# Weight slots of 2304 bytes: the 64-byte shift moves from the activation sums to the weights of the seven-product jobs

## The chip, the cores and the metric

The kernel runs on one core of a Trainium2 chip. The metric is the device time of one execution in microseconds (us); a lower time is better. The kernel before was timed three times: 955.7, 956.73 and 957.67 us, so its median is 956.73 us.

## What is computed

One layer of a decoder for 512 positions of width 1024, in float32:

```python
h = rmsnorm(x, norm_mix_g)
bg, cg, xv, q, k, v, z, a, b, ga, gb = split(h @ w_in)
y_a = (bg * causal_dwconv(cg * xv, conv_a_w)) @ w_a_out
y_b = gdn_branch(q, k, v, z, a, b, ...) @ w_b_out      # gated delta rule, 8 heads, chunks
x = x + (sigmoid(ga) * y_a + sigmoid(gb) * y_b) @ w_o
h = rmsnorm(x, norm_ffn_g)
gate, val = split(causal_dwconv(h @ w_up, ffn_conv_w))
x = x + (silu(gate) * val) @ w_down
out = rmsnorm(x, norm_final_g)
```

The products with `w_in`, `w_up`, `w_o`, `w_down`, `w_a_out` and `w_b_out` make up nearly all of the work.

## The kernel before

**Three matmuls for one.** Each float32 operand of a large product is split into a rounded part (type fp32r) and the rest, and a product becomes high times low, low times high and high times high (`mm3`, `times`). Activations are split once (`hT`, `h2`, `yas`, `yb`, `mix`, `xs`; the trace names `h2` as `h`). Weights are split as they pass: a block of 1 MB is loaded by an SP DMA into one of two `raw` tiles, and `Block.part` lets ACT round each quarter of 2048 bytes per partition into a `wh` slot (line 140) and DVE subtract it into a `wl` slot (line 141). There are `WQ` = 12 slots of each kind, used in a ring: a quarter's slot is written again when TensorE has read it for the last time. SP, ACT and DVE each take their instructions in order.

**Jobs.** `run_jobs` walks a list of pairs (block, use). During job i, one step of the split of block i+1 is put out at each tick, and a tick falls after every 2048 streamed columns (`mm`). Loads are issued some jobs ahead. There are three kinds of jobs:

- `col_job`: a 256-column block of weights against all 512 positions, 48 matmuls with 512 streamed columns and the weights stationary. Its block has four quarters.
- `sum_job`: the same result by seven products of half-size blocks instead of eight (Winograd's form of Strassen's method). Each product is 12 matmuls with 256 streamed columns, so a job has 84. Its block (`SumBlock`) splits seven parts, "11", "22", "s2", "s1", "s3", "s4" and "12". Three of the products, "11", "s4" and "12", stream quarters of the activations themselves (`hT` or `h`), and the other four stream the sums of such quarters, which `activation_sums` makes once for each stage: the tiles `ts` in the first stage and `us` in the stage of `w_up`. There are ten sum jobs in the first stage (three each of `w_in`'s columns cg, bg and ga, and one of xv) and eight in the stage of `w_up`.
- the jobs of `w_o` and `w_down` (`FormBlock`, `times_a`, `times_b`): activations are stationary here, and the weights stream with 512 columns.

**Where tiles lie.** In bytes within a partition, the program before has the `wh` slots from 19424 on and the `wl` slots from 44000 on, 2048 apart; the halves of `hT` at 68576 and 84960, those of `h` at 84960 and 101344; the tiles of `ts` at 134624 and 151264 and those of `us` at 151008 and 167648. All these numbers leave 224 when divided by 256. `place` makes the tiles of `ts` and `us`, which are 64 elements longer than their contents; for these two names alone the contents begin `UP` = 48 elements (192 bytes) into the tile:

```python
UP = 48
def place(pool_, tag, name, up=0):
    t = pool_.tile([P, ND * S + 64], F32R, tag=tag, name=name)[:, up:up + ND * S]
```

So the distance from the address of a streamed quarter of `hT` or `h` to that of any weight of 128 columns is a multiple of 256 bytes, and for `ts` and `us` it is 192 more than a multiple of 256.

**Between the stages.** The last jobs of `w_o` finish rows of x, normalise them (`fin1`), turn them on TensorE and write `h` (lines 1375 and 1376). The first two blocks of `w_up` are used together by `first_val`, on one half of the positions and then on the other, with 256 streamed columns. `activation_sums` (lines 251, 258, 260 and 261) then makes `us`.

**The order on each engine.** The code puts instructions out as the queues of tasks advance at ticks, and the framework's planner orders each engine's instructions by its own costs except where the code says otherwise.

Of the kernel before, what the change touches and what calls it, by code (L numbers as in the profile page):

```python
# [28 lines left out]
Y_V, Y_T, Y_G, Y_N, Y_E, SLAB = 4, 17, 16, 3, 4, 4  # L29
Y_F = (5, 4, 6, 3)  # L30
WARM = 3
WQ = 12
FEED = 3
Y_M = 10

# [25 lines left out]
def layer_kernel(ctx, tc, x, norm_mix_g, w_in, w_ab, conv_a_w, gdn_conv_w, gdn_A_log, gdn_dt_bias,  # L61
# [60 lines left out]
            mm(o, ah, bh, False, i == n - 1, free)  # L122


    class Block:
        def __init__(self, src, quarter=(4, P)):
            self.src, self.quarter = src, quarter
            self.raw, self.ready, self.lead, self.fed = None, False, 2, True
            self.wh, self.wl = {}, {}
# [5 lines left out]
            nc.sync.dma_start(out=self.raw, in_=self.src())  # L135

        def part(self, name, src):
            wh = self.wh[name] = wp.tile([P, *self.quarter], F32R, tag="wh", bufs=WQ, name=nm("wh"))
            wl = self.wl[name] = wp.tile([P, *self.quarter], F32R, tag="wl", bufs=WQ, name=nm("wl"))
            act.copy(out=wh, in_=src)  # L140
            dve.tensor_tensor(out=wl, in0=src, in1=wh.bitcast(F32), op=ALU.subtract)  # L141

# [8 lines left out]


    class SumBlock(Block):
        def split(self):
            if self.ready:
                return
            self.ready = True
            r = [self.raw[:, q] for q in range(4)]

            def to(q, a, b, op):  # L160
                dve.tensor_tensor(out=r[q], in0=a, in1=b, op=op)  # L161

            self.part("11", r[0])
            yield
            self.part("22", r[2])
            yield
            to(2, r[3], r[2], ALU.add)
            to(3, r[0], r[3], ALU.subtract)
            yield
            to(0, r[2], r[0], ALU.subtract)  # L170
            self.part("s2", r[0])
            yield
            self.part("s1", r[2])
            yield
            self.part("s3", r[3])
            yield
            to(0, r[1], r[0], ALU.subtract)
            self.part("s4", r[0])
            yield
            self.part("12", r[1])  # L180
            yield
# [146 lines left out]
        return SumBlock(lambda: w[i]), use  # L328


    UP = 48

    def place(pool_, tag, name, up=0):
        t = pool_.tile([P, ND * S + 64], F32R, tag=tag, name=name)[:, up:up + ND * S]
        return t.rearrange("p (m a n) -> p m a n", m=4, a=4)

    def by_rows(t):
# [101 lines left out]
    with tc.tile_pool(name="st1", bufs=1) as st1:  # L439
# [83 lines left out]
                                     op0=ALU.mult, op1=ALU.subtract)  # L523

        def round_k(q):
            wh = k_block.wh[q] = wp.tile([P, 4, P], F32R, tag="wh", bufs=WQ, name=nm("wh"))
            act.copy(out=wh, in_=k_block.raw[:, q])

        def rest_k(q):
            wl = k_block.wl[q] = wp.tile([P, 4, P], F32R, tag="wl", bufs=WQ, name=nm("wl"))  # L530
            dve.tensor_tensor(out=wl, in0=k_block.raw[:, q], in1=k_block.wh[q].bitcast(F32), op=ALU.subtract)


# [89 lines left out]
    def gates_chain(o):  # L623
        abT = gd.tile([P, S], F32, tag="cv", bufs=2, name="abT")[0:32]
        act.copy(out=abT, in_=o[0:32, :])
        yield
        o2 = bank()
        for n in range(NT):
            pe.transpose(out=o2[:, n * 32:(n + 1) * 32], in_=abT[:, n * P:(n + 1) * P], identity=ident[:32, :32])
        ab4 = o2[:, 0:128].rearrange("p (n c) -> p c n", c=32)  # L630
        abv = gd.tile([P, 16, NT], F32, name="abv")
        dve.tensor_copy(out=abv, in_=ab4[:, 16:32])
        dve.tensor_tensor(out=abv, in0=abv, in1=ab4[:, 0:16], op=ALU.add)
        T = lambda n: gd.tile([P, 32], F32, tag=n, name=nm(n))
        u, t, z, q, g = T("u"), T("t"), T("z"), T("q"), T("g")
        dve.tensor_tensor(out=hn(u), in0=abv[:, 0:8, :], in1=dtb.unsqueeze(2).broadcast_to([P, H, NT]), op=ALU.add)
        tc.keep_in_program_order(act.activation(out=hn(beta), in_=abv[:, 8:16, :], func=AF.Exp, scale=-1.0))
        tc.keep_in_program_order(act.activation(out=alg, in_=alg, func=AF.Exp))
        dve.tensor_scalar(t, u, -1.0, None, op0=ALU.mult)
        dve.tensor_tensor(out=t, in0=t, in1=u, op=ALU.min)  # L640
        tc.keep_in_program_order(act.activation(out=t, in_=t, func=AF.Exp))
        yield
        pool.tensor_scalar(beta, beta, 1.0, None, op0=ALU.add)
        pool.tensor_scalar(z, t, 2.0, None, op0=ALU.add)
        yield
        dve.reciprocal(out=beta, in_=beta)
        dve.reciprocal(out=z, in_=z)
        dve.tensor_scalar(u, u, 0.0, None, op0=ALU.max)
        yield
        pool.tensor_tensor(out=t, in0=t, in1=z, op=ALU.mult)  # L650
        pool.tensor_tensor(out=z, in0=t, in1=t, op=ALU.mult)
        pool.tensor_scalar(q, z, 1.0 / 15.0, 1.0 / 13.0, op0=ALU.mult, op1=ALU.add)
        for c in (11, 9, 7, 5, 3, 1):
            pool.tensor_tensor(out=q, in0=q, in1=z, op=ALU.mult)
            pool.tensor_scalar(q, q, 1.0 / c, None, op0=ALU.add)
        pool.tensor_tensor(out=q, in0=q, in1=t, op=ALU.mult)
        pool.tensor_scalar(q, q, 2.0, None, op0=ALU.mult)
        pool.tensor_tensor(out=g, in0=q, in1=u, op=ALU.add)
        pool.tensor_tensor(out=hn(g), in0=hn(g), in1=alg.unsqueeze(2).broadcast_to([P, H, NT]), op=ALU.mult)
        pool.tensor_scalar(g, g, -1.0, None, op0=ALU.mult)  # L660
        for _ in range(Y_G):
            yield
        o3 = bank()
        pe.matmul(o3[:, 0:32], lhsT=triu, rhs=g, start=True, stop=True)
        pe.matmul(o3[:, 32:64], lhsT=ones, rhs=g, start=True, stop=True)
        G, Gl = T("G"), T("Gl")
        dve.tensor_copy(out=G, in_=o3[:, 0:32])
        dve.tensor_copy(out=Gl, in_=o3[:, 32:64])
        dve.tensor_scalar(negG, G, -1.0, None, op0=ALU.mult)
        dve.tensor_tensor(out=kdv, in0=Gl, in1=G, op=ALU.subtract)  # L670
        act.activation(out=kdv, in_=kdv, func=AF.Exp)
        act.activation(out=eGl, in_=Gl, func=AF.Exp)
        act.activation(out=eG, in_=G, func=AF.Exp)
        dve.tensor_scalar(neG, eG, -1.0, None, op0=ALU.mult)
        yield
        o4 = bank()
        pe.transpose(out=o4[0:32, 0:P], in_=G, identity=ident)
        GT = gd.tile([32, P], F32, name="GT")
        dve.tensor_copy(out=GT, in_=o4[0:32, 0:P])
        nc.sync.dma_start(out=gtd, in_=GT)  # L680
        prep(0)
# [22 lines left out]
    def front(pr, st):  # L704
# [72 lines left out]

        dve.tensor_tensor(out=TB, in0=UB.rearrange("p j i -> p i j"), in1=nlow, op=ALU.mult)
        dve.memset(TB.rearrange("p i j -> p (i j)")[:, ::17], 1.0)
        sub = tl("sub", 1, (64, 64))  # L780
        for j in range(1, 15):
            m = 15 - j
            t = sub[:, 0:m * j].rearrange("p (i c) -> p i c", c=j)
# [333 lines left out]
    def open_conv():  # L1117
        drain(evacs)
        drain(chains)
        drain(mids)  # L1120
        drain(backs)
        p2.close()
        sc = st["sc"] = p3.enter_context(tc.tile_pool(name="sc", bufs=1, side="right"))
        st["ts"] = [place(sc, f"t{i}", f"ts{i}", UP) for i in range(2)]
        st["ya"] = sc.tile([P, ND, S], F32, name="ya")
        room["pool"] = sc
        adds.extend((Task(o_w.form()), Task(down_w.form())))
        sums_of.append(Task(activation_sums(hT, st["ts"], sc.tile([P, ND, S], F32, tag="mixa", name="xf"))))
# [99 lines left out]
    def wb_c(g):  # L1228
        def c(j, o):
            m = 2 * g + j  # L1230
            t, mix = tmp("t"), st["mixa"][:, m, :]
            dve.tensor_tensor(out=t, in0=o, in1=sgb[0][:, m, :], op=ALU.mult)
            dve.tensor_tensor(out=mix, in0=t, in1=mix, op=ALU.add)
            yield
            if j == 1 and g % 2 == 1:
                if g == 1:
                    st["mix"] = [place(st["sc"], f"t{i}", f"mix{i}") for i in range(2)]
                yield from prep_a(mix_pairs(g - 1), st["mix"], g - 1)
        return c
# [189 lines left out]
    def open_up():  # L1429
        p7.close()  # L1430
        p3.close()
        up = st["up"] = ctx.enter_context(tc.tile_pool(name="up", bufs=1, side="right"))
        cvp = st["cvp"] = ctx.enter_context(tc.tile_pool(name="cvp", bufs=2))
        room["pool"], room["o"] = cvp, 2
        st["ts"] = [place(up, f"t{i}", f"us{i}", UP) for i in range(2)]
        st["aT"] = [up.tile([P, NA, S], F32, name="aTa")]
        xf = up.tile([P, ND, S], F32, tag="late", name="xf2")
        st["gfn"] = cvp.tile([P, D], F32, name="gfn", bufs=1)
        nc.sync.dma_start(out=st["gfn"], in_=norm_final_g.partition_broadcast(P))
        return xf  # L1440
# [277 lines left out]
```

## Time and profile before

| | |
|---|---|
| median of three runs | 956.73 us |
| span of the profiled execution | 954.4 us |
| time around the span (the difference) | 2.3 us |
| TensorE (PE) busy | 943.3 us, 99% |
| weight loads (PEld) busy | 817.3 us, 86% |
| VectorE (DVE) busy | 741.9 us, 78% |
| ScalarE (ACT) busy | 510.0 us, 53% |
| GpSimd (POOL) busy | 161.0 us, 17% |

A row of the timeline begins with the start in us from the beginning of the span and the length; engine, line, operation, output and inputs, shape and count follow, and in brackets the idle time before it with what ended it. A matmul's length includes the time that it overlaps with the next one, so the distance from one start to the next is what a matmul costs. In a row of the chain the first number is the start and the second the length. In a row of waits stand who waited for whom, the total in us, how often, and the longest.

### The profile page before, as it was taken

How to read it: one execution, taken by the hardware profiler on the slowest of the kernel's cores; microseconds unless marked ns; L12 is line 12 of the kernel's file. 1: busy time of each engine (PE TensorE's matmuls, PEld its weight loads, DVE VectorE, ACT ScalarE, POOL GpSimd, SP SyncE). 2: the span in 40 equal slices, each digit the busy share in tenths (PEclk: the TensorE clock that was granted, in tenths of full speed). 3: DMA queues.
4: the chain of work that ended last, by engine and by line, in shares of the span. 5: the costliest groups of instructions: out<-in, count | busy, mean ns of one | idle time of the engine just before them, and what ended most of it. 6: DMA issues, size and time to landing. Idle time of an engine off the chain costs nothing.

```text
span 954.4 us, 16266 instructions
## 1 busy us (share of the span) xinstructions
PE 943.3 (99%) x6188; PEld 817.3 (86%) x6188; DVE 741.9 (78%) x1401; ACT 510.0 (53%) x1105; POOL 161.0 (17%) x280
## 2 busy tenths in 40 slices
PE   8999999999999999999999999999999999999997
PEld 6888887987878889999988888988889998888885
DVE  5878686896625967899863479999988888969785
ACT  6895756575453434444642145555645456556463
POOL 3330401303010211321231100231222210000000
PEclk9999999999999999999999999999999999999999
DMA  6443312222222447657786445594774783176332
GB/s 229 156 141 104 114 53 90 76 78 74 60 84 75 125 122 159 164 158 180 244 256 154 124 136 197 173 231 157 169 191 166 196 161 133 45 267 229 100 133 89
DMA packets 51887, 138.13 MB, mean 145 GB/s; under 512 B 21691, under 2 KB 22624, under 8 KB 43104
## 3 DMA queue, kind: packets, MB, share of 16 engines
q1 hardware_dynamic: 39120, 107.45, 33.0%
q0 software_dynamic: 12544, 29.37, 16.1%
q8 instruction: 49, 0.80, 0.3%
q14 instruction: 30, 0.25, 0.1%
q10 hardware_dynamic: 144, 0.26, 0.1%
HBM read 133.64 MB, written 32.78 MB: 174 GB/s over the span
## 4 chain that ended last, share of the span: by engine, by line
PE 90%; DVE 4%; ACT 2%; issue 1%; POOL 1%; POOLq 0%
PE ps L108 83%; PE ps L701 1%; PE ps L736 1%; DVE wl L141 1%; PE ps L939 1%; PE ps L959 1%; DVE hn L1362 1%; DVE h L1376 1%; PE ps L948 0%; PE ps L927 0%; PE ps L926 0%; POOL r L1360 0%; PE ps L823 0%; DVE x L1355 0%; ACT junk L766 0%
## 5 line engine op out<-in xcount | busy, mean ns | idle before, releaser
L108 PE MATMUL ps<-hT,wh 128*128 128x512 f32 (+1 forms) x1104 | 318.4, 368 | 0.3 <-DVE hT L521 0.3
L140 ACT CAST wh<-raw 128x512 fp32r<-128x512 f32 x350 | 202.9, 618 | 215.4 <-PE ps L108 135.3
L141 DVE TENSOR_TENSOR wl<-raw,wh 128x512 fp32r<-128x512 f32 x350 | 230.9, 684 | 54.6 <-ACT wh L140 53.6
L108 PEld LDWEIGHTS ps<-hT,wh 128*128 128x128 f32 x1104 | 196.6, 189 | 28.9 <-DVE hT L521 0.5
L108 PE MATMUL ps<-hT,wl 128*128 128x512 f32 (+1 forms) x552 | 195.0, 361 | 0.0
L108 PE MATMUL ps<-h,wh 128*128 128x512 f32 (+1 forms) x704 | 177.7, 341 | 0.3 <-DVE h L1376 0.3
L108 PEld LDWEIGHTS ps<-h,wh 128*128 128x128 f32 x704 | 122.3, 189 | 15.6 <-DVE h L1376 0.5
L108 PEld LDWEIGHTS ps<-hT,wl 128*128 128x128 f32 x552 | 104.3, 189 | 13.8
L108 PE MATMUL ps<-h,wl 128*128 128x512 f32 (+1 forms) x352 | 114.5, 341 | 0.0
L108 PE MATMUL ps<-wh,xs 128*128 128x512 f32 (+1 forms) x320 | 96.7, 384 | 0.0
L108 PEld LDWEIGHTS ps<-h,wl 128*128 128x128 f32 x352 | 66.6, 189 | 7.6
L108 PEld LDWEIGHTS ps<-wh,xs 128*128 128x128 f32 x320 | 59.6, 188 | 11.8
L108 PE MATMUL ps<-wl,xs 128*128 128x512 f32 (+1 forms) x160 | 61.4, 384 | 0.0
L223 POOL COPY gate<-raw 1x1 f32<-1x1 f32 x38 | 13.5, 355 | 273.1 <-DMA raw<-in_w_in_dram 120.4
L108 PE MATMUL ps<-ts,wh 128*128 128x256 f32 x320 | 56.2, 276 | 0.0
L348 DVE SCALAR_TENSOR_TENSOR cv<-ps,wA,cv 128x511 f32<-128x511 f32 (+2 forms) x72 | 53.1, 740 | 3.7 <-ACT cv L345 3.5
L140 ACT CAST wh<-raws 128x512 fp32r<-128x512 f32 x66 | 39.2, 619 | 26.1 <-PE ps L108 8.7
L141 DVE TENSOR_TENSOR wl<-raws,wh 128x512 fp32r<-128x512 f32 x66 | 42.8, 685 | 12.1 <-ACT wh L140 12.1
L161 DVE TENSOR_TENSOR raw<-raw 128x512 f32<-128x512 f32 x72 | 49.3, 685 | 1.4
L108 PEld LDWEIGHTS ps<-ts,wh 128*128 128x128 f32 x320 | 49.0, 188 | 0.0
L108 PE MATMUL ps<-us,wh 128*128 128x256 f32 x256 | 45.0, 276 | 0.0
L108 PE MATMUL ps<-yas,wh 128*128 128x512 f32 x128 | 39.6, 389 | 0.0
(333 smaller groups left out, 1568.1 us busy)
## 6 DMA issues: line engine op xcount, KB each, us to landing
raw<-in_w_in_dram SPq DMA_DIRECT2D x35, 1024.0 KB, 5.2
raw<-in_w_up_dram SPq DMA_DIRECT2D x22, 1024.0 KB, 5.0
dv<-in_w_down_dram POOLq DMA_DIRECT2D x50, 256.0 KB, 6.2
raws<-dv SPq DMA_DIRECT2D x8, 768.0 KB, 5.6
ov<-in_w_o_dram POOLq DMA_DIRECT2D x20, 256.0 KB, 5.2
raws<-in_w_down_dram SPq DMA_DIRECT2D x10, 512.0 KB, 6.0
raw<-in_w_a_out_dram SPq DMA_DIRECT2D x4, 1024.0 KB
raw<-in_w_b_out_dram SPq DMA_DIRECT2D x4, 1024.0 KB, 5.1
```

Source lines behind the costliest of these rows:

```text
L108: pe.matmul(o, lhsT=a, rhs=b, start=start, stop=stop, skip_group_check=free)
L140: act.copy(out=wh, in_=src)
L141: dve.tensor_tensor(out=wl, in0=src, in1=wh.bitcast(F32), op=ALU.subtract)
L161: dve.tensor_tensor(out=r[q], in0=a, in1=b, op=op)
L223: tc.keep_in_program_order(pool.tensor_copy(out=gate[:, 0:1], in_=el[:, 0:1]))
L348: dve.scalar_tensor_tensor(out=dst[:, sh:], in0=src[:, :S - sh], scalar=wcol(j), in1=dst[:, sh:], op0=ALU.mult, op1=ALU.add)
L701: pe.transpose(out=o[:, n * P:(n + 1) * P], in_=src[:, n * P:(n + 1) * P], identity=ident)
L736: pe.matmul(o[:, i], lhsT=kqs[:, a, h, 0, sl], rhs=kqs[:, b, h, :, sl], start=a > 0, stop=a + b == 0)
L939: pe.matmul(o[:, 0:P], lhsT=TTf[:, f, :], rhs=rs[h], start=True, stop=True)
L959: pe.matmul(o[:, 0:P], lhsT=A[:, f, :], rhs=vns[h], start=True, stop=True)
L1362: dve.scalar_tensor_tensor(out=hn_[:, sl], in0=x1[:, t, sl], scalar=r, in1=st["gff"][:, sl], op0=ALU.mult, op1=ALU.mult)
L1376: dve.tensor_tensor(out=h2[1][:, 4 * g:4 * g + 4, t * P:(t + 1) * P], in0=ov, in1=hs.bitcast(F32), op=ALU.subtract)
```

## The change

Weight slots become 576 elements (2304 bytes) long, and `SumBlock` sets `shift = 16`: its seven parts lie 16 elements (64 bytes) into their slots. Other blocks keep a shift of 0. The tiles of `ts` and `us`, and all others made by `place`, lose the 64 spare elements and the offset of 48. The ring shrinks from 12 to 11 slots of each kind. Two small tiles share memory with others: `abv` of `gates_chain` takes the tag `sub`, and the temporary of `wb_c` takes the tag `c`.

```diff
-WQ = 12
+WQ = 11
...
+    def slot(tag, quarter, shift=0):
+        t = wp.tile([P, S + 64], F32R, tag=tag, bufs=WQ, name=nm(tag))[:, shift:shift + S]
+        return t.rearrange("p (k n) -> p k n", k=quarter[0]) if len(quarter) > 1 else t
+
     class Block:
+        shift = 0
+
...
         def part(self, name, src):
-            wh = self.wh[name] = wp.tile([P, *self.quarter], F32R, tag="wh", bufs=WQ, name=nm("wh"))
-            wl = self.wl[name] = wp.tile([P, *self.quarter], F32R, tag="wl", bufs=WQ, name=nm("wl"))
+            wh = self.wh[name] = slot("wh", self.quarter, self.shift)
+            wl = self.wl[name] = slot("wl", self.quarter, self.shift)
...
     class SumBlock(Block):
+        shift = 16
+
...
-    UP = 48
-
-    def place(pool_, tag, name, up=0):
-        t = pool_.tile([P, ND * S + 64], F32R, tag=tag, name=name)[:, up:up + ND * S]
+    def place(pool_, tag, name):
+        t = pool_.tile([P, ND * S], F32R, tag=tag, name=name)
         return t.rearrange("p (m a n) -> p m a n", m=4, a=4)
...
-        abv = gd.tile([P, 16, NT], F32, name="abv")
+        abv = gd.tile([P, 16, NT], F32, tag="sub", name="abv")
...
-        sub = tl("sub", 1, (64, 64))
+        sub = tl("sub", 1, (P, 64))[0:64]
...
-        st["ts"] = [place(sc, f"t{i}", f"ts{i}", UP) for i in range(2)]
+        st["ts"] = [place(sc, f"t{i}", f"ts{i}") for i in range(2)]
...
-            t, mix = tmp("t"), st["mixa"][:, m, :]
+            t, mix = tmp("c"), st["mixa"][:, m, :]
...
-        st["ts"] = [place(up, f"t{i}", f"us{i}", UP) for i in range(2)]
+        st["ts"] = [place(up, f"t{i}", f"us{i}") for i in range(2)]
```

`round_k` and `rest_k`, which split the first block by hand, take their slots from `slot` as well, without a shift.

More of the change, by code (lines that the diff above doesn't have):

```diff
@@ L525, in round_k @@
         def round_k(q):
-            wh = k_block.wh[q] = wp.tile([P, 4, P], F32R, tag="wh", bufs=WQ, name=nm("wh"))
+            wh = k_block.wh[q] = slot("wh", (4, P))
             act.copy(out=wh, in_=k_block.raw[:, q])
         def rest_k(q):
-            wl = k_block.wl[q] = wp.tile([P, 4, P], F32R, tag="wl", bufs=WQ, name=nm("wl"))
+            wl = k_block.wl[q] = slot("wl", (4, P))
             dve.tensor_tensor(out=wl, in0=k_block.raw[:, q], in1=k_block.wh[q].bitcast(F32), op=ALU.subtract)
```

## Prediction

> **What bounds the kernel now.** I read the page first (engines, granted clock), then the chain that ended last, then TensorE's waits in the long stretches of that chain, then the matmul groups by shape, and last the timeline of one seven-product job.
>
> ```profile
> span 954.4 us, 16266 instructions
> PE 943.3 (99%) x6188; PEld 817.3 (86%) x6188; DVE 741.9 (78%) x1401; ACT 510.0 (53%) x1105; POOL 161.0 (17%) x280
> PEclk9999999999999999999999999999999999999999
> 308.55 279.25 PE ps L108 x1641
> 621.35 316.90 PE ps L108 x1765
> PE ps L108 <- DVE h L1376: 0.3, 1, 0.3
> ```
>
> The clock is full everywhere. The two chain rows are stretches, 308.55 to 587.8 and 621.35 to 938.25, in which the chain is nothing but TensorE's matmuls of line 108. The last row is the only wait of TensorE from 308.6 on, at 621.35. All 18 seven-product jobs lie in these stretches, so what a matmul there costs, from one start to the next, goes one to one into the time.
>
> ```profile
> L108 PE MATMUL ps<-h,wh 128*128 128x256 f32 x320 | 60.7, 284 | 0.3 <-DVE h L1376 0.3
> L108 PE MATMUL ps<-hT,wh 128*128 128x256 f32 x304 | 58.9, 284 | 0.3 <-DVE hT L521 0.3
> L108 PE MATMUL ps<-ts,wh 128*128 128x256 f32 x320 | 56.2, 276 | 0.0
> L108 PE MATMUL ps<-us,wh 128*128 128x256 f32 x256 | 45.0, 276 | 0.0
> L108 PEld LDWEIGHTS ps<-us,wh 128*128 128x128 f32 x29 | 4.3, 188 | 0.0
> L108 PEld LDWEIGHTS ps<-h,wh 128*128 128x128 f32 x13 | 1.9, 192 | 0.0
> ```
>
> The first four rows are all of the kernel; the last two are weight loads within one job, beside `us` and beside `h`. The same shape of matmul takes 276 ns with the shifted sums and 284 with activations, and its weight load 188 ns against 192. Both streams are longer together, which speaks for the two of them getting in each other's way, rather than for a slow operand. A job has 32 `wh` products of sums (4 products of 12, two thirds of them with `wh`), so 320/32 = 10 jobs and 256/32 = 8 jobs: the 18.
>
> ```profile
> 655.23 0.29 PE L108 MATMUL ps<-us,wh 128*128 128x256 f32 x1
> 657.51 0.73 PE L108 MATMUL ps<-us,wh 128*128 128x256 f32 x5
> 658.87 0.73 PE L108 MATMUL ps<-us,wh 128*128 128x256 f32 x5
> 660.23 0.62 PE L108 MATMUL ps<-us,wh 128*128 128x256 f32 x4
> 660.69 0.28 PE L108 MATMUL ps<-h,wh 128*128 128x256 f32 x1
> 661.63 0.76 PE L108 MATMUL ps<-h,wh 128*128 128x256 f32 x5
> 663.07 0.88 PE L108 MATMUL ps<-h,wh 128*128 128x256 f32 x5
> ...
> 653.80:663.55 9.75, 9.75 (x86) 9.75 (x84) 8.95 (x17) 2.57 (x5) 1.73 (x4) 1.00 0.67 226
> 663.55:674.46 10.91, 10.91 (x51) 9.02 (x50) 10.76 (x18) 8.18 (x15) 2.04 (x4) 1.00 0.50 148
> ```
>
> This is the first seven-product job of `w_up`. From 657.51 to 658.87 and on to 660.23 a group of 12 products of sums takes 1.36 us, 113.3 ns each. From 661.63 to 663.07 a group of 12 products of activations takes 1.44 us, 120.0 ns each. The 48 sums from 655.23 to 660.69 take 5.46 us (113.75 each, as the first few still come slowly), the whole job 9.75 us, and the other 36 products the rest, 4.29 us (119.2 each, as the first few after the sums come faster). The last two rows are that job and the four-quarter job behind it (span, then PE, PEld, DVE busy).
>
> **The change part by part.**
>
> *The shift.* What differs between the two kinds of product is the distance from the streamed operand to the weights that load meanwhile: 0 modulo 256 bytes for `hT` and `h`, 192 for `ts` and `us`. After the change the sums lie unshifted and the weights 64 bytes on, so all seven products have a distance of -64, which is 192 modulo 256: for the sums it stays, for the 36 others it turns from 0 to 192. Slots of 2304 bytes (nine times 256) add 256 in odd slots. Modulo 2048 the products of sums before have already met 192 plus every multiple of 256, as the two tiles of sums lie 256 modulo 512 apart and parts step by 512, and all ran at 113 to 114 ns. So no distance occurs in a sum job afterwards that was not seen fast before. A job then costs 84 x 113.3 ns = 9.52 us instead of 9.75, less about 0.01 where the first products still come slowly: 0.22 us saved, times 18 jobs = **4.0 us**. Bounds: if the others reach only the 117.5 ns of the eight products right behind the sums (660.69 to 661.63, 0.94 us), 18 x 36 x 1.7 ns = 1.1 us; if the settling goes too, 4.2. I take 4.0, as the steady rows are the nearest.
>
> *Who must keep up.* DVE is busy 8.95 + 10.76 = 19.71 of the 20.66 us of the two jobs above. The pair will last 20.44, still above 19.71.
>
> *Other products.* Blocks without a shift keep a distance of 0 modulo 256, in odd slots 256 modulo 512. With `w_o`, where the weights stream against `mix`, whose halves lie 0 and 256 modulo 512 away from the slots, the spacing is even:
>
> ```profile
> 584.45 0.39 PE L108 MATMUL ps<-wl,mix 128*128 128x512 f32 x1
> 585.13 0.39 PE L108 MATMUL ps<-wl,mix 128*128 128x512 f32 x1
> ```
>
> Three matmuls, of both halves, in 0.68 us, 226.7 each, as for `hT` and `h`. I cost it at nothing.
>
> *Shared tiles.* `abv` is read for the last time in the first chain task, before `front` runs and writes `sub`; the last readers of the tag `c` (line 1167) are past before the `w_b_out` jobs write it. No wait, no cost.
>
> *The ring of 11.* ACT already waits for slots, and each wait now is for a quarter one later.
>
> ```profile
> ACT wh L140 <- PE ps L108: 144.0, 68, 4.7
> 694.86 0.62 ACT L140 CAST wh<-raw 128x512 fp32r<-128x512 f32 x1 [3.72 <-PE ps L108]
> 695.51 0.69 DVE L141 TENSOR_TENSOR wl<-raw,wh 128x512 fp32r<-128x512 f32 x1 [1.70 <-ACT wh L140]
> 704.39 0.88 PE L108 MATMUL ps<-h,wh 128*128 128x256 f32 x5
> ```
>
> The cast at 694.86 waited 3.72 us for its slot, and DVE ended that block's split at 696.2; TensorE starts the block's job at about 704.9 (four products before it in the last row). So a split that waited this long still comes 8.7 us early, and the slot that it would wait for instead is freed at most half a four-quarter job (10.91/2 = 5.5 us) later. What is queued behind a waiting cast are first taps of convolutions, whose PSUM banks TensorE needs back later: no such wait shows before. Cost nil in the steady part.
>
> One place differs, the turn to `w_up`. There the first two blocks are used together and hold eight slots, and the third block's four fill all 12:
>
> ```profile
> 613.08 2.18 ACT L140 CAST wh<-raw 128x512 fp32r<-128x512 f32 x4
> 617.56 0.68 DVE L141 TENSOR_TENSOR wl<-raw,wh 128x512 fp32r<-128x512 f32 x1
> 619.47 1.22 DVE L251 TENSOR_TENSOR xf<-h,h 128x1024 f32<-128x1024 f32 x1
> 620.61 0.68 DVE L1376 TENSOR_TENSOR h<-ps,h 128x512 fp32r<-128x512 f32 x1
> 620.79 0.28 PE L108 MATMUL ps<-h,wl 128*128 128x256 f32 x1
> 621.35 0.39 PE L108 MATMUL ps<-h,wh 128*128 128x256 f32 x1 [0.28 <-DVE h L1376]
> 624.17 0.62 ACT L140 CAST wh<-raw 128x512 fp32r<-128x512 f32 x1 [4.38 <-DMA raw<-in_w_up_dram]
> 651.60 1.21 DVE L261 TENSOR_TENSOR us<-xf,us 128x1024 fp32r<-128x1024 f32 x1
> 600.00:650.00 50.00, 49.72 (x323) 45.20 (x322) 48.24 (x73) 29.48 (x52) 12.62 (x19) 1.00 0.67 179
> ```
>
> With 11 slots the last of the four casts must wait until the first block's first quarter has been read for the last time, some 14 products into the part that starts again at 621.35, about 623. That takes the subtraction at 617.56 (0.60 us) out of DVE's way ahead of the last `h`: the gap at 620.79 to 621.35, 0.44 over the usual 0.12, can go. That is the gain end, -0.44. But the `raw` tile is freed at about 624.3 and not at 618.24, so the next block lands about 6 us later than 624.17, and four subtractions (2.4 us) move behind convolutions and sums. The tight place is `us`: its last half is written at 652.81 and first read by the products from 655.23, 2.4 us later. DVE is busy 48.24 of these 50 us. Were it to idle all 6 us, TensorE would stand 6.1 - 2.4 = 3.7 us: the loss end. DVE has four convolutions and the making of the sums to fill the gap with, which need no block, so I take a value near the gain end, +0.3.
>
> *Sum.* -4.0 + 0.3 = -3.7 us: a span of 950.7, and with the 2.3 us that lie between the span and the median of runs, **953.0 us** against 956.73.
>
> **The rivals.**
>
> *The ring gives it back* (17%). The 3.7 us stall above would leave 956.4; casts that hold up ACT's queue elsewhere as well, a microsecond more, 957.4; from 5.9 us in all it would be slower. For it: 68 waits, and the thin 2.4 us ahead of `us`. Against it: TensorE waited for no weights once, with ACT 53% busy.
>
> *The distance is not the cause* (5%): something else in the sums makes them fast, the 36 stay at 120 and the sums at 113. Then the ring's +0.3 is left: 957.0. Against it: shape, count and weights are the same; only the tile differs. The Trainium skill would have it so: "TensorE: Matmul & The Clock Gate", Step-by-step, gives TensorE two independent read ports, so that loading the next weights takes nothing from a running matmul; by that no offset matters, and the time would be this rival's. The loads' 188 and 192 ns beside the matmuls' 276 and 284 disagree with it.
>
> *The streamed tile's own place decides* (7%), the other side. `ts` and `us` are fast because they begin 192 bytes on, whatever the weights do. Then the shift of the weights gives nothing, and the unshifted sums go to 120: 18 x (84 x 120 ns - 9.75 us) = +5.9 us, so 962.6 and with the ring 962.9. It decides once the sums lose 2.2 ns each (864 x 2.2 ns = 1.9 us) with nothing won. For it: before, all weights lay alike, so the trace can't part the two. Against it: the weight loads lengthen too, which a stream that was slow by its own address would not explain.
>
> **How the numbers follow.** The forecast has 71% (951 to 954.7); the first rival 17%, of it 4 under 954.8, 8 within and 5 over 958.6; the second 5% (no change); the third 7% (slower). Against 0.2% (1.9 us, about what a measurement of this kernel can tell from no change) that is faster 0.75, same 0.13, slower 0.12. The range goes from 951.0 (956.73 - 4.2 - 0.44 and the 1.0 by which the runs before spread downwards) to 957.2 (the ring's loss and the second rival); the likeliest case alone has 951.0 to 954.7.
>
> **What would show it.** In the profile after, groups of 12 products of `h` and `hT` in seven-product jobs 1.36 us long, their matmuls at 276 ns and loads at 188; those of sums unchanged; seven-product jobs 9.53 us long; still no wait of TensorE from about 625 to the end, or none over 1 us at the first products of `us`; the block behind `first_val` landing near 630. Products of `h` at 120 would prove the shift idle, sums at 120 the third rival, and waits for `wl`, `us` or banks the first.

## The result and the profile after

The changed kernel takes 962.11 us (median of four runs, 961.43 to 963.1) against 956.58 for the kernel before on the same chip: a ratio of 1.0062, 95% interval 1.0049 to 1.0074. It is slower by 5.5 us; 953.0 was predicted. The profiled execution has a span of 961.4 us. First its page, two rows of TensorE's waits, and the groups of matmuls by shape with the weight loads of `us`:

```profile
span 961.4 us, 16258 instructions
PE 946.6 (98%) x6188; PEld 820.5 (85%) x6188; DVE 746.2 (78%) x1401; ACT 509.1 (53%) x1103; POOL 165.1 (17%) x280
...
PE ps L108 <- DVE kn L728: 2.9, 1, 2.9
PE ps L108 <- DVE us L269: 0.2, 1, 0.2
...
L108 PE MATMUL ps<-h,wh 128*128 128x256 f32 x320 | 60.3, 283 | 0.0
L108 PE MATMUL ps<-hT,wh 128*128 128x256 f32 x304 | 58.3, 282 | 0.8 <-ACT hT L523 0.5 <-DVE hT L527 0.3
L108 PE MATMUL ps<-ts,wh 128*128 128x256 f32 x320 | 58.2, 281 | 0.0
L108 PE MATMUL ps<-us,wh 128*128 128x256 f32 x256 | 46.6, 281 | 0.2 <-DVE us L269 0.2
L108 PEld LDWEIGHTS ps<-us,wh 128*128 128x128 f32 x256 | 39.8, 189 | 0.3 <-issue 0.3
```

Two things are new. TensorE waits 2.9 us for `kn`, a tile of the first chain pair. And the products of sums went from 276 to 281 ns, while those of activations only went from 284 to 283 and 282. The timeline of the second seven-product job of `w_up` shows the pace; each row is a stretch of five `wh` products in a row, and two such rows in sequence begin twelve products apart:

```profile
682.86 0.75 PE L108 MATMUL ps<-us,wh 128*128 128x256 f32 x5
684.27 0.75 PE L108 MATMUL ps<-us,wh 128*128 128x256 f32 x5
685.69 0.75 PE L108 MATMUL ps<-us,wh 128*128 128x256 f32 x5
...
688.51 0.75 PE L108 MATMUL ps<-h,wh 128*128 128x256 f32 x5
689.93 0.87 PE L108 MATMUL ps<-h,wh 128*128 128x256 f32 x5
```

Twelve products take 1.41 to 1.42 us, with sums and with activations alike. From start to start that is 117.8 ns for all 84, where 113.3 was predicted for all, and where before the settled paces were 113.3 for the 48 sums and 120.0 for the other 36. A job grows by 0.14 us (84 x 117.8 ns = 9.89 against 9.75), the 18 jobs by 2.5 us.

Matched product by product, TensorE's starts are 0.3 us late ahead of 56 us and 5.0 us late from 74 us on: 4.7 us arise in between. Here are two windows of the changed kernel (span, then PE, PEld, DVE, ACT and POOL busy, granted clock), and its timeline on TensorE, ScalarE and VectorE; the last two rows are ScalarE of the kernel before:

```profile
56.00:60.00 4.00, 1.16 (x10) 0.83 (x8) 2.66 (x5) 3.90 (x17) 0.00 (x0) 1.00 0.10 41
60.00:64.00 4.00, 3.91 (x10) 3.12 (x11) 3.90 (x15) 2.55 (x13) 2.01 (x1) 0.57 0.01 4
...
56.12 1.03 PE L707 MATMUL ps<-ident,kq 128*128 128x128 f32 x8
60.09 0.50 PE L108 MATMUL ps<-hT,wh 128*128 128x512 f32 x1 [2.93 <-DVE kn L728]
60.43 0.48 PE L108 MATMUL ps<-hT,wl 128*128 128x512 f32 x1
63.69 0.54 PE L108 MATMUL ps<-hT,wl 128*128 128x512 f32 x1
64.30 0.40 PE L108 MATMUL ps<-hT,wl 128*128 128x512 f32 x1
64.53 0.40 PE L108 MATMUL ps<-hT,wh 128*128 128x512 f32 x1
...
51.80 2.45 ACT L624 ACTIVATE Dm<-Dm,negG 128x128 f32<-128x128 f32 x8 [0.27 <-POOL Dm L616]
54.16 0.26 ACT L727 ACTIVATE junk<-ps 128x128 f32<-128x128 f32 x1
54.53 1.28 ACT L1020 ACT_TABLE_LOAD   x1
58.71 0.30 ACT L727 ACTIVATE junk<-ps 128x128 f32<-128x128 f32 x1
59.35 0.68 DVE L728 TENSOR_TENSOR kn<-ps,kdv 128x512 f32<-128x512 f32 x1
```
```profile
53.04 0.28 ACT L721 ACTIVATE junk<-ps 128x128 f32<-128x128 f32 x1
56.66 2.45 ACT L618 ACTIVATE Dm<-Dm,negG 128x128 f32<-128x128 f32 x8
```

Before, the eight squares of `ssk` were done at 53.3 and the exponentials of `Dm` came behind them, at 56.66. After, the exponentials and a table load stand in ScalarE's queue ahead of the last squares, which end at 59; VectorE's second `kn` runs at 59.35, and TensorE's next product waits 2.93 us for it. Then the granted clock falls to 0.57: the nine products from 60.43 come 0.41 us apart (3.26 us for eight steps) instead of 0.23. Wait and slow clock are some 2.9 + 1.7 us, nearly all of the 4.7. The Trainium skill ("TensorE: Matmul & The Clock Gate", Part 1) has the clock fall to half after an idle window of some 3.4 us; here the idle time was 2.93 us, behind 1.0 us of nothing but transposes (the row at 56.12), so the trace agrees only if the transposes count as idle too, which no run here separates.

The profiled execution was the slowest of the four, 7.0 us over the profiled one before. Matched in the same way, 0.3 us of it lie ahead of 56 us, 4.7 in this stall, 2.5 in the seven-product jobs and 0.1 at the turn to `w_up`; 0.6 are won back between 200 and 250 us.

### The profile page after: what moved, and what is told of

Same layout as the page of the kernel before. It is cut to its first block, busy times and chain, and to the rows that moved or that the text cites. A ratio compares the mean times of both kernels' runs of the same rounds, so it can differ in the third digit from the quotient of the medians.

```text
span 961.4 us, 16258 instructions
## 1 busy us (share of the span) xinstructions
PE 946.6 (98%) x6188; PEld 820.5 (85%) x6188; DVE 746.2 (78%) x1401; ACT 509.1 (53%) x1103; POOL 165.1 (17%) x280
## 4 chain that ended last, share of the span: by engine, by line
PE 92%; ACT 2%; DVE 2%; DMA 1%; POOL 0%; issue 0%; POOLq 0%
PE ps L108 85%; PE ps L707 1%; PE ps L742 1%; PE ps L945 1%; PE ps L965 1%; ACT Dm L624 1%; PE ps L954 0%; PE ps L933 0%; PE ps L932 0%; PE ps L1377 0%; DMA Dm<-gtd 0%; PE ps L829 0%; PE ps L838 0%; PE ps L907 0%; DVE wl L147 0%
## 5 line engine op out<-in xcount | busy, mean ns | idle before, releaser
L147 DVE TENSOR_TENSOR wl<-raw,wh 128x512 fp32r<-128x512 f32 x350 | 233.8, 690 | 50.6 <-ACT wh L146 48.6
L231 POOL COPY gate<-raw 1x1 f32<-1x1 f32 x38 | 16.2, 427 | 289.9 <-DMA raw<-in_w_in_dram 119.4
L108 PE MATMUL ps<-ts,wh 128*128 128x256 f32 x320 | 58.2, 281 | 0.0
L108 PEld LDWEIGHTS ps<-us,wh 128*128 128x128 f32 x256 | 39.8, 189 | 0.3 <-issue 0.3
```

The lines of the kernel that those rows point to most:

```text
L108: pe.matmul(o, lhsT=a, rhs=b, start=start, stop=stop, skip_group_check=free)
L231: tc.keep_in_program_order(pool.tensor_copy(out=gate[:, 0:1], in_=el[:, 0:1]))
```

## The experiments

Each ratio is against the kernel before on the same chip. "Late exponentials" is the edit of the second experiment. Places are bytes modulo 256, as (streamed, weights).

| kernel | median us | ratio | 95% interval |
|---|---|---|---|
| ring of 11 alone | 960.9 | 1.0046 | 1.0033 to 1.0059 |
| the same, late exponentials | 955.4 | 0.9998 | 0.9989 to 1.0007 |
| changed, late exponentials | 958.17 | 1.0021 | 1.0012 to 1.0030 |
| changed, sums shifted and not weights | 959.41 | 1.0039 | 1.0025 to 1.0053 |
| changed, 12 slots of 2112 bytes | 968.06 | 1.0127 | 1.0113 to 1.0140 |
| before, `hT` and `h` shifted too | 960.27 | 1.0043 | 1.0029 to 1.0057 |
| changed, weights shifted by 192 bytes | 962.24 | 1.0068 | 1.0054 to 1.0081 |
| before, all 32 bytes on | 955.73 | 1.0001 | 0.9992 to 1.0010 |
| before, sums shifted by 64 and 128 | 959.68 | 1.0042 | 1.0028 to 1.0057 |
| late exp., `11` unshifted | 957.74 | 1.0019 | 1.0010 to 1.0028 |
| late exp., sums and last two shifted by 64 | 954.82 | 0.9989 | 0.9980 to 0.9997 |
| late exp., `11` at 128 bytes | 953.69 | 0.9976 | 0.9966 to 0.9986 |
| late exp., sums and last two by 192 | 953.19 | 0.9974 | 0.9965 to 0.9983 |
| late exp., `11` at 192 bytes (one run) | 954.54 | | |

### The early stall

**The ring of 11 alone.** Kernel before, `-WQ = 12`, `+WQ = 11`.

> The kernel before with one edit, 11 slots instead of 12 (slots of 2048 bytes, weights and sums where they were). Theory R (the ring reorders the first chain pair's work on ScalarE and VectorE, and that makes the stall near 57 us): some 4.9 us of delay arise between 56 and 69 us as in the changed kernel, with a wait of TensorE for `kn` of nearly 3 us and a clock under 0.7 in the 4 us behind it; seven-product jobs stay at 9.75 us; time 956.6 + 4.6 to 5.2 = 961.2 to 961.8. Rival L (the stall comes from the new places of the tiles, or from the shared tiles `abv` and `sub`): no wait for `kn`, 956.3 to 957.2, the ring costing at most the 0.4 us at the turn to `w_up`.

Measured 960.9, just under theory R's range. Its two new waits of TensorE:

```profile
PE ps L108 <- DVE kn L722: 2.7, 1, 2.7
PE ps L108 <- DVE us L261: 1.0, 1, 1.0
```

The stall is there with every tile in its old place (2.7 us, then a clock of 0.67 from 60 to 64; 4.4 us arise in this stretch), so the ring makes it, and not the new places. The wait for `us` is the turn to `w_up`, of which more below. Jobs stay at 9.75 us but for one.

**Late exponentials.** The ring of 11 with this edit in `front`:

```diff
-        if pr == 0:
-            exps(0)
-        Dm = Dms.pop(pr)
+        Dm = Dms[pr]
 ...
             yield
+        if pr == 0:
+            exps(0)
+        Dms.pop(pr)
         dve.tensor_scalar(sk, ssk, EPS, None, op0=ALU.add)
```

> The ring of 11 alone (as in the second kernel of this study's first experiment, 960.9 us) with one more edit: in `front` of the first pair the eight exponentials of `Dm` are issued behind the squares of `ssk` instead of ahead of them. Theory Q (the stall near 57 us is those exponentials, which wait for `Dm`, standing in ScalarE's queue ahead of four squares): the wait for `kn` goes, the clock stays at full, and of the 4.8 us of delay that the ring made before 69 us at least 4 go; what is left is the ring's cost at the turn to `w_up`, about 1.4 us in that run: 956.1 + 0.5 to 1.6 = 956.6 to 957.7. Rival C (the ring starves TensorE of weight slots in that stretch, and the order is a bystander): a wait of similar length moves to `wh` or `wl`, 960 to 961.5.

Measured 955.4, no difference from the kernel before, and under the 956.6 to 957.7 of theory Q.

```profile
52.54 2.44 ACT L618 ACTIVATE Dm<-Dm,negG 128x128 f32<-128x128 f32 x8
53.44 0.68 DVE L720 TENSOR_TENSOR kn<-ps,kdv 128x512 f32<-128x512 f32 x1
56.16 0.48 PE L108 MATMUL ps<-hT,wh 128*128 128x512 f32 x1
```

The squares now end ahead of the exponentials, `kn` is written at 53.44, and TensorE goes on at 56.16 at a clock of 1.00. All that the ring cost (4.8 us against the kernel before on its chip) is gone with the ring still at 11: theory Q. What the ring did was to alter the order that the planner chose. The edit also moved some other instructions of ScalarE, VectorE and TensorE, all in the same early stretch. That the time fell further than expected comes from the turn to `w_up`: its wait isn't in this execution, though the order of instructions there is that of the ring of 11 alone.

**The changed kernel with late exponentials.** The same edit in the changed kernel.

> The changed kernel with the eight exponentials of the first pair issued behind the squares, and nothing else. If the loss of 5.5 us is the stall (order of ScalarE's queue) plus the pace of 117.8 ns, the two add: the ring's part goes as it did with the ring alone (955.4), and 18 x 0.14 = 2.5 us stay: 957.9, between 957 and 959. Were the two linked (the stall also made by the places of the tiles), 960 or more.

Measured 958.17, in the expected range. The two parts add: 0.0041 of the ratio (3.9 us) was the stall, and against the ring of 11 with the same edit 2.2 us stay by the ratios, for 2.5 of pace.

### What the places do

**Sums shifted and not weights**, in the changed kernel: `-shift = 16`, `+shift = 0` in `SumBlock`, and `UP = 48` for `ts` and `us` as before.

> The changed kernel (11 slots of 2304 bytes, shared tiles) with weights not shifted and the sums' tiles 192 bytes on again, as before the change. Instructions stand in the order of the changed kernel. Expected if the pace is set by places modulo 256: sums at 113.3 ns, quarters of `h` and `hT` at 120.0, jobs 9.75 us, as before; the stall near 57 us stays; time about 956.6 + 4.9 = 961.5, less than the changed kernel by 0 to 1 us in spite of 18 x 0.14 = 2.5 us fewer in jobs only if something else grows, else 959.6 (962.1 - 2.5). If the pitch of 2304 bytes itself slows products: jobs over 9.75.

Measured 959.41. Sums at 113.7 ns, quarters at 119.3 on the mean, jobs 9.75 us: slots of 2304 bytes cost nothing, and what lies between this kernel and the changed one (2.2 us by the ratios) is the move of the shift.

**Slots of 2112 bytes, 12 of them**, in the changed kernel: `-WQ = 11`, `+WQ = 12`, and `S + 16` for `S + 64` in `slot`.

> The changed kernel with slots of 2112 bytes and 12 of them (the same bytes in all), everything else as changed: weights of seven-product jobs 64 bytes in, sums not shifted. Slots now begin in 64-byte steps modulo 256. Theory R: no stall near 57 us, and what is left of the loss is the pace of the seven-product jobs, about 117.8 ns per product: 956.6 + 18 x 0.14 = 959.1, between 958.5 and 960. Rival L (new places or shared tiles make the stall): the wait for `kn` stays and the time is 961 to 962.5. Theory W (the place of the weights modulo 256 alone sets the pace, once the streamed tile is fixed at 224): quarters differ by their slot, 120.0 ns at weights 224 and 117.8 at 32, others unknown, and the mean job lies between 9.5 and 10.0 us. Theory S (only the streamed tile's place counts): every slot gives one and the same pace.

Measured 968.06, a miss. The stall is gone and the order that of before, but the 512-column products, whose weights now lie at four different places, went from 226.7 to some 231.5 ns. The streamed tile is always at 224. A part's `wh` and `wl` slots can now lie at different places; where both lie alike, groups of twelve came out mostly at 120.0 with weights at 224, at an unsettled 118 to 120 with 96, and at either 113.3 or 117.8 with 32 and with 160. One pair of places with two paces was the first sign that places alone don't decide.

**`hT` and `h` shifted too**, in the kernel before: their tiles get 64 spare elements and begin 48 elements in, as `ts` and `us` do.

> The kernel before (12 slots of 2048 bytes, weights not shifted, sums' tiles 192 bytes on) with `hT` and the final `h` also 192 bytes on. Order of instructions as before. Theory P (the pair of places decides; streamed at 160, weights at 224 modulo 256 gives 113.3 ns, as for the sums before): all 84 products at 113.3 ns, jobs 9.53 us, 956.6 - 18 x 0.22 = 952.6 at least; the 512-column products of these tiles, 226.7 ns so far, have never been seen with a distance of 192, and if they gain the same 6.7 ns each the time falls far more, toward 940. Rival D (sums are fast for another reason than their place): quarters stay at 120.0 and the time at 956.6.

Measured 960.27: half of theory P. The products of seven-product jobs settle at 113.3 ns in 125 of 126 groups of twelve (the other one follows a stop of 0.04 us), activations as well as sums: in the first two rows eighteen products of `h` take 2.04 us. But the 512-column products of these tiles lose as much each: in the other four rows fourteen take 3.27 us here (233.6 ns) and 3.17 us in the kernel before (226.4).

```profile
684.17 0.28 PE L108 MATMUL ps<-h,wh 128*128 128x256 f32 x1
686.21 0.28 PE L108 MATMUL ps<-h,wh 128*128 128x256 f32 x1
...
331.20 0.39 PE L108 MATMUL ps<-hT,wl 128*128 128x512 f32 x1
334.47 0.39 PE L108 MATMUL ps<-hT,wl 128*128 128x512 f32 x1
```
```profile
327.67 0.39 PE L108 MATMUL ps<-hT,wl 128*128 128x512 f32 x1
330.84 0.39 PE L108 MATMUL ps<-hT,wl 128*128 128x512 f32 x1
```

So the place of the streamed tile against the weights matters, for activations as for sums, and of these two the better one differs with the length of the stream: -64 for 256 columns, 0 for 512.

**All 32 bytes on**, in the kernel before: a 32-byte longer `phalf` moves slots and activations, `up` 8 elements more the rest.

> The kernel before with every weight slot, `hT`, `h` and the other streamed tiles 32 bytes further on, so that they begin at 0 and not at 224 modulo 256 (sums at 192, still 64 below); all differences between places are kept. Theory O (only the differences count): quarters 120.0, sums 113.3, 512-column products 226.7 ns, 956.1. Theory A (the absolute place counts too, as the changed kernel's 117.8 at the same differences suggests): paces move; each nanosecond on the 2784 512-column products is 2.8 us and on the 1512 products of seven-product jobs 1.5 us, so anything from 930 to 970.

Measured 955.73, with 120.0, 113.7 and 226.7 ns as before: theory O. The absolute place doesn't count by 32 bytes.

**Sums shifted by 64 (`ts`) and 128 bytes (`us`)**, in the kernel before: `UP` replaced by 16 and by 32.

> The kernel before with the sums' tiles 64 bytes on in the first stage (`ts` at 32 modulo 256, weights at 224) and 128 bytes on in `w_up` (`us` at 96) instead of 192 in both. A map of the streamed tile's place with the weights fixed. Theory B or M: -64 (as before) is 113.3, 0 is 120.0; 64 on and 128 on are not seen with weights at 224. If 64 on mirrors -64: `ts` at 113.3; if 128 on is worst: `us` near 122. Quarters stay at 120.0. Each ns on `ts` is 0.48 us, on `us` 0.38 us; 954 to 964.

Measured 959.68. `ts` runs at a settled 117.8, `us` at 118.8 with single products from 115 to 122; the quarters of `h` and `hT` stay at 120. So +64, entered from the 120.0 of equal places, is not the mirror of the -64 of before, which gave 113.3 from there.

**Weights shifted by 192 bytes**, in the changed kernel: `-shift = 16`, `+shift = 48`.

> The changed kernel with the weights of seven-product jobs 192 bytes into their slot instead of 64, so at 160 modulo 256 where the streamed tiles are at 224. In the kernel with slots of 2112 bytes the groups with weights at 160 ran at 113.3 to 118, those at 32 at 113.3 in some places and 118 in others. Theory B (what a pair of places gives depends on the pace it is entered from, with two paces that hold themselves): 113.3 or about 118 for whole jobs. If 113.3: 962.1 - 18 x 84 x 4.5 ns = 955.3. If 118: 962. Theory M (the mirror place is another case, distance 64 and not -64): a third pace, between 113 and 122, time between 955 and 968.

Measured 962.24, all 126 groups at 117.8. With weights at 160 and at 32 the pace is the same, with streamed tiles at 224 and a difference of +64 and of -64.

### The way in

In the ring of 11 alone, every place modulo 256 is that of the kernel before, and so is every pair (160, 224) of the sums. Yet its first job of `w_up`, which comes behind the wait for `us`, differs from all others (first three rows; the last two are the next job):

```profile
659.84 0.36 PE L108 MATMUL ps<-us,wh 128*128 128x256 f32 x1 [1.00 <-DVE us L261]
660.86 0.75 PE L108 MATMUL ps<-us,wh 128*128 128x256 f32 x5
662.27 0.75 PE L108 MATMUL ps<-us,wh 128*128 128x256 f32 x5
...
681.72 0.73 PE L108 MATMUL ps<-us,wh 128*128 128x256 f32 x5
683.08 0.73 PE L108 MATMUL ps<-us,wh 128*128 128x256 f32 x5
```

Twelve products take 1.41 us in the one and 1.36 in the other: 117.8 and 113.3 ns, same tile, same places, one kernel. All 48 sums of that job keep the slow pace. So there are two paces at this difference, each holds itself, and what goes before has a part in the choice: here a stop of TensorE. The five runs that follow vary what goes before.

**`11` unshifted** (late exponentials): `part` takes `self.shift if name != "11" else 0`.

> The kernel of the run before this one (changed, exponentials late) with the first of the seven products of a job, the one with weights `11`, left unshifted, so that a job enters at equal places (120 ns) and the six others follow at weights 32, streamed 224. Theory B (two paces that hold themselves; the entry chooses): coming from 256-column products at equal places, as the sums before the change did and 12 of 15 such groups of the 2112-byte kernel, the six run at 113.3, a job costs 12 x 119.5 + 72 x 113.3 = 9.59 us, time 955.4 - 18 x (9.75 - 9.59) = 952.5. Theory N (shifted weights are slow whatever comes first, 3 of 15 groups): 117.8 stays, 120 + 117.8: job 9.92, time 958.4.

Measured 957.74. Theory B's forecast fell: all 18 jobs go on at 117.8 behind the settled 120.0 of `11`. In the 2112-byte kernel the three groups at 32 that came from a settled 120.0 had done so too. Followed slot by slot, eighteen others took 113.3: ten of them came from an unsettled pace, but five came from a settled 117.8 with weights at 160, and the expectations here count no such group.

**Sums and the last two shifted** (late exponentials): `UP = 48` for the sums; weights of `s4` and `12` by 64 bytes, others by 0.

> Ring of 11 with 2304-byte slots and late exponentials; the sums' tiles 192 bytes on as before the change, and only the weights of a job's last two products (`s4`, `12`) shifted by 64 bytes; its first (`11`) unshifted. So the first quarter is at equal places (120), the four sums at streamed 160 and weights 224, the last two quarters at streamed 224 and weights 32: the same difference of -64 throughout those six. Theory B: the last two take over the 113.3 of the sums, job 9.59 us, 952.5 as in the run before. Theory N (a shift of the weights is not what a shift of the streamed tile is): 24 products at 117.8, 12 at 120, 48 at 113.3: job 9.70, time 955.4 - 18 x 0.05 = 954.5.

Measured 954.82, theory N's 954.5. The sums run at 113.3 (again but for the job behind a wait for `us`, 117.8), the last two products at 117.8: streamed tile and weights both move by 64 bytes, the difference stays, and the fast pace is lost.

**`11` at 128 bytes, the other six at 64** (late exponentials).

> As the run with the first product of a job unshifted (ring of 11, late exponentials), but the weights `11` 128 bytes into their slot (at 96 modulo 256, streamed 224), the other six at 64 bytes. In the kernel with 2112-byte slots, all 12 groups that came to weights at 32 from an unsettled pace (118.8 ns on the mean, single products from 112 to 123) took 113.3, and the 3 that came from a settled 120.0 took 117.8, as did all 18 here. Theory B (the entry chooses): the six run at 113.3; job 12 x 118.8 + 72 x 113.3 = 9.58 us; 958.2 (the run with the late exponentials alone) - 18 x (9.89 - 9.58) = 952.6. Theory N (shifted weights with this pitch are slow whatever the entry): 117.8 stays, 958.

**Sums shifted, last two by 192 bytes** (late exponentials).

> As the run that shifted only the weights of a job's last two products (954.8), with 192 bytes for them instead of 64. The sums go at 113.3; where the difference changed by nothing, from -64 by moving streamed tile and weights together, the pace fell to 117.8; where it jumped by 128, in the kernel of 2112-byte slots from weights at 32 to 160 under a streamed tile at 224, all 5 groups kept 113.3. Theory B: here it jumps by 128 too (-64 to +64), the last two keep 113.3; job 12 x 119.5 + 72 x 113.3 = 9.59 us against 9.72, 954.8 - 18 x 0.12 = 952.6. Theory N: 117.8 stays, 954.8.

**`11` at 192 bytes, the other six at 64** (late exponentials).

> As the first of these three, with the weights `11` 192 bytes into their slot (at 160). In the run with all weights at 160 that pace was a settled 117.8, so theory B has the six others enter from a settled slow pace and stay at 117.8 (job 9.89 us, 958); if they come out at 113.3 the jump of 128 by itself brings the fast pace (9.59 us, 952.7), which would be a simpler rule.

Measured 953.69, 953.19 and 954.54 (the last one a single run), against expectations of 952.6, 952.6 and 952.7 for the fast pace. The first two are faster than the kernel before by 0.24% and 0.26%. The second job of `w_up` in the first of the three:

```profile
676.03 0.73 PE L108 MATMUL ps<-us,wh 128*128 128x256 f32 x5
677.39 0.73 PE L108 MATMUL ps<-us,wh 128*128 128x256 f32 x5
...
680.11 0.73 PE L108 MATMUL ps<-h,wh 128*128 128x256 f32 x5
681.47 0.85 PE L108 MATMUL ps<-h,wh 128*128 128x256 f32 x5
```

Sums and activations at 1.36 us for twelve, at the very places, (224, 32), where the changed kernel takes 1.41. Of the 108 groups of twelve other than `11`, 106 run at 113.3, though only the weights of `11` differ from the changed kernel with late exponentials (958.17). In the second kernel it is 101 of 108, in the third 102. Every slow group of the three, at 117.8, follows a stop of TensorE within its job: six each in the second and third behind the wait of 0.9 to 1.0 us for `us`, three at the end of the first stage behind stops of 0.07 to 0.4 us (what a stop adds from start to start).

A stop doesn't always bring the slow pace. At the end of the first stage the third kernel has two stops of 0.4 and 0.5 us, and 113.3 is back within six products; in the first three rows, behind the second of them, seven products take 0.79 us. The changed kernel with sums shifted and not weights goes on at 113.3 behind a stop of 0.13 us.

```profile
465.67 0.38 PE L108 MATMUL ps<-hT,wh 128*128 128x256 f32 x1 [0.22 <-DVE u L301]
465.89 0.28 PE L108 MATMUL ps<-hT,wl 128*128 128x256 f32 x1
466.68 0.85 PE L108 MATMUL ps<-hT,wh 128*128 128x256 f32 x5
```
```profile
657.13 0.75 PE L108 MATMUL ps<-us,wh 128*128 128x256 f32 x5
658.54 0.75 PE L108 MATMUL ps<-us,wh 128*128 128x256 f32 x5
...
661.38 0.75 PE L108 MATMUL ps<-h,wh 128*128 128x256 f32 x5
662.79 0.87 PE L108 MATMUL ps<-h,wh 128*128 128x256 f32 x5
```

Nor does theory B hold throughout. In ten jobs of the third kernel `11` runs at a settled 117.8 and no stop follows; in all ten the weights' jump by 128 bytes under the same streamed place brings 113.3, as in the five groups of the 2112-byte kernel. But a jump of the difference by 128 bytes is no rule either. In the second kernel's first job of `w_up` (the last four rows) the sums stand at 117.8 behind the stop, the last two products change the difference from -64 to +64 by moving both operands, and they stay at 117.8. And in the first kernel the difference jumps by 64 only, from 128 to -64, and the pace is fast in all 18 jobs, where the jump by 64 from equal places gave the slow one in all 18. So what goes before matters (957.74 and 953.69 us differ in nothing but the weights of `11`), but no rule tried here foretells every case, and what inside the chip holds a pace wasn't tried.

## Why the prediction was wrong, point by point

**The shift** (-4.0 us predicted, +2.5 measured). The step that failed is "no distance occurs in a sum job afterwards that was not seen fast before". The distances were as worked out, and a distance of -64 does allow 113.3 ns: quarters took it in the kernel with `hT` and `h` shifted. But the distance doesn't fix the pace. Reached by moving the streamed tile under fixed weights, as the sums did before the change, it gave 113.3. Reached by moving the weights by 64 bytes away from equal places, as the change does, it gave 117.8 (126 of 126 groups), which none of the rows before showed. The quoted rows held a hint: the first products behind a switch ran at another pace than their place later had, which was put down to settling instead of read as a state carried over. The bound of 117.5 ns for the 36 was near what they got, by chance: it was the pace of eight products on their way to 120.0. That the 48 would lose 4.5 ns each was in no bound of this term. Why a moved weight and a moved streamed tile differ at the same distance stays open.

**The ring** (nil in the steady part predicted; some 4.7 us from 56 us on measured). The step that failed is "One place differs, the turn to `w_up`". "Each wait now is for a quarter one later" priced waits in the second half, where they are indeed hidden: behind the stall TensorE waits for no weight slot. Left out was that the ring enters the planner's order. One edit that puts the exponentials back behind the squares took the ring's whole cost away.

**The turn to `w_up`** (+0.3 predicted, -0.44 to 3.7 as bounds). The mechanism came as described, and the price is near, in part by luck:

```profile
638.79 0.62 ACT L146 CAST wh<-raw 128x512 fp32r<-128x512 f32 x1 [2.04 <-DMA raw<-in_w_up_dram]
640.98 0.75 DVE L354 SCALAR_TENSOR_TENSOR v<-ps,wF,v 128x511 f32<-128x511 f32 x1 [2.59 <-ACT v L351]
661.04 0.36 PE L108 MATMUL ps<-us,wh 128*128 128x256 f32 x1 [0.16 <-DVE us L269]
```

The block lands late (its first cast at 638.79, not near 630, though TensorE was 5.5 us behind by then), ScalarE's queue stands, VectorE idles 2.59 us, and the 2.4 us of slack ahead of `us` are used up with 0.16 us of wait left. Matched product by product, the gap at 621 us gave 0.3 us back, and the first job of `w_up` lost 0.4: +0.1. In five other kernels with 11 slots the same wait is 0.9 to 1.0 us, in the rest there is none, and two with one order of instructions, the changed kernel with late exponentials (0.9) and the same with `11` unshifted (none), differ in it. What makes the wait vary stays open.

**Other products and shared tiles** (nil): right. 512-column products keep 226.7 ns with slots 0 and 256 modulo 512 apart, and the ring of 11 alone has the same order of instructions as the changed kernel. **Who must keep up**: right for this kernel, where TensorE waits for no weights in these jobs. With the fast pace the margin is thinner than the pair of jobs showed: in a run of seven-product jobs one behind the other, the row at 465.67 above is a wait for VectorE's `u`.

**The rivals.** The third gave 962.6 to 962.9 and the time came out there, but for another reason: the sums went to 117.8 and not to 120, and the quarters changed too. It is refuted by the run with `11` at 128 bytes, where activations and sums streamed from the unshifted 224 took 113.3. The kernel with `hT` and `h` shifted refutes the second rival, since there activations were as fast as sums. The two independent read ports of the Trainium skill ("TensorE: Matmul & The Clock Gate", Step-by-step), by which no place would matter, don't account for 113.3, 117.8 and 120.0 ns. The first rival named the right part of the change, the ring, with the wrong place and mechanism.

## What to carry to other kernels

A buffer ring that is shortened where nothing waits can still cost time, because it changes the order that a planner gives an engine's queue: compare the order of instructions, and look first at the stage where TensorE hangs on a short chain of other engines, since a stall near 3 us there brought a slow clock on top. Where the pace of a product depends on the places of its operands, take the pace from groups entered in the same way, and read the first products behind each switch as part of the evidence. A place that is best for one length of stream may be the worse one for another.

## What the runs showed of the hardware

- Products of 256 streamed fp32r columns have settled spacings of 113.3, 117.8 and 120.0 ns. Equal places modulo 256 gave 120.0, differences of -64 and +64 gave 113.3 or 117.8, 128 gave an unsettled 118 to 121 on the mean of twelve.
- At differences of 64 the two paces hold themselves through whole jobs. A move of the weights by 64 bytes gave the slow one from the 120.0 of equal places (18 of 18 jobs) and the fast one from the unsettled pace at a difference of 128 (18 of 18). A move of the weights by 128 bytes, from 160 to 32, led from a settled 117.8 to 113.3 (15 of 15 groups).
- Of eleven stops of TensorE (0.04 to 1.2 us) within jobs that else run at 113.3, eight were followed by the slow pace and three by the fast one.
- 512-column products go at 226.7 ns at equal places and at some 233 at -64, the other way round.
- A wait of 2.93 us of TensorE was followed by 3.6 us with products 0.41 us apart instead of 0.23.
